# A hybrid attention layer on one core: the in-projection's dense keys normalized in one block, its finishing steps and sums dealt out anew

## The chip, the cores and the metric

The kernel runs on one core of one Trainium2 chip. The metric is device time in microseconds (us); the time before is the median of three runs. A core has TensorE (PE in the profile; its weight loads are PEld), VectorE (DVE), ScalarE (ACT), GpSimd (POOL) and SyncE (SP), which here issues nearly all DMAs. Each engine works through its own queue in order, and the queues meet at semaphores. PE writes its sums to PSUM, eight banks of 512 float32 for each of 128 partitions; what DVE, ACT and DMAs share otherwise is SBUF.

## The reference

One encoder layer on 1024 positions of width 1024. Cut to the part at hand:

```
proj = rms_norm(x, norm1_g) @ w_in            # (1024, 2304) -> qA 512 | kA 128 | vA 128 | qB 512 | kB 512 | vB 512
qa = apply_axial_rope(rms_norm(qa, qa_norm_g))   # 8 heads of 64
ka = apply_axial_rope(rms_norm(ka, ka_norm_g))   # 2 heads, used by 4 query heads each
out_a = softmax(qa @ ka.T / 8) @ va
out_b = dilated_mixture_attention(rms_norm(qb, qb_norm_g), rms_norm(kb, kb_norm_g), vb)
x = x + concat(rms_norm(out_a), rms_norm(out_b)) @ w_out
x = x + conv_ffn(rms_norm(x, norm2_g), w_up, conv_w, conv_b, w_down)
```

The keys and values of mixer A (kA, vA, 256 columns) are called dense here, those of mixer B dilated. qb_norm_g and kb_norm_g each multiply one side of the same inner product over the 64 elements of a head.

## The kernel before

All is in one function, `tile_encoder_layer`, which unrolls everything; its parts are small nested functions. Three arenas hold all data: `bigf` (float32), `bigr` (a float32 form for PE) and `ps` (PSUM); places are offsets such as `F_TMP` or `qab(t)`, and several stages use one place in turn. For the order of the work the kernel leaves it to a planner: from a planned time of each instruction and from what each reads and writes, it lays out the queue of each engine when the program is built. The text gives priorities, not the order: of the instructions that the planner takes to be ready, the one that comes first in the text goes first. At run time each queue is in order, whatever is late.

Products are made exact by splitting: an operand becomes a high part (ACT copy into `bigr`) and the rest (DVE subtraction), and three matmuls are added (L393 to L395: high x high, high x rest, rest x high).

The in-projection runs in these steps.

*Dense keys and values.* For each of eight tiles of 128 positions (`kv_proj`, L278 to L280) 24 matmuls give 256 columns in a PSUM bank (`kv_bank`: banks 0 to 3, then 2 and 3 in turn). `kv_stage1` squares the 128 key columns on ACT, sums them on DVE and takes the root on ACT (L291 to L294). `kv_stage2` finishes the reciprocal root (`newton`, L190 to L193, DVE), multiplies the keys (L302), builds a table of rope and gain (L304, POOL), multiplies by the cosines (L305), turns the halves (`rot`, L284, POOL), adds (L308), copies the values out of PSUM (L309, ACT) and writes the tile to DRAM (`kvscr`, L310). `x_prep` and `x_rest` between them transpose x (L179) and split it (L227, L228) and make the differences of halves (L249 to L253) that the products below need; `s_split` splits these.

*Four chunks of 512 columns*, in the order kB, vB, qA, qB (chunk 0 to 3). Each chunk is a 2 x 2 block product done with seven block products instead of eight, so there are 28 products (`prods`, numbered by `m`; the list at `prods` gives which of the seven, n, each one is). A product is 48 matmuls of 256 columns over four tiles, into one of three groups of two PSUM banks (`in_group`). Product n = 2 adds onto the group of n = 1, after ACT has copied that out (L408). `in_out(m)` takes a product out of PSUM and adds it to the block's outputs at `c_at`; at n = 6 four sums follow, two on DVE and two on POOL (L405 is the line of all sums). `w_prep(m + 2)` prepares the weights two products ahead: a difference of weight blocks (L366 DVE, L368, L370, L372 POOL), the high part (L376, ACT) and the rest (L377, DVE). `w_load` and `w_scale` (L353) bring the next chunk's weights; the places for the first half are used by every second chunk (`F_WA`).

*Finishing steps.* When a quarter of a chunk is complete, `done` returns its steps as a list: square (L463 to L465), root (L470 and `newton`), norm (L474), and then for kB the gain (L490, POOL) and the DMAs out (L494), for qA a table (L477, POOL), four turns (L284), cosine (L484) and add (L487); for vB a scaling on ACT (L444) and DMAs (L445). The main loop runs the whole list of a quarter after the product that follows its completion; of two quarters of qA three steps only, and all of qB's, are left for the attention that follows.

*Dense keys for attention.* In chunk 3 the tiles come back from DRAM two at a time (`kv_fetch`, L313), are split (`k_ready`: L319, L320), transposed by PE (L176) and copied (L326, L327); `v_ready` (L333) scales the values, `fill_k` (L337) fills constants. `a_prep(0)` prepares the first queries: its steps are `first`, four maxima `mx` (L582, L583) and `last`. Attention A then runs 16 groups (`a_main`), each of which takes the steps of the next group's `a_prep` by a plan, one number for each of its eight key tiles.

Names for the prediction's steps: `F_TMP` holds 1024 columns of scratch, `F_WA[1]` the first half of the weights of chunks 1 and 3 (and, before chunk 1, the places `F_KVT` and `F_CST`), `SM_R1` the positions' own norm factors for the values.

Of the kernel before, what the change touches and what calls it, by code (L numbers as in the profile page):

```python
# [20 lines left out]
HD = 64  # L21
# [37 lines left out]
R_KNA = 3072  # L59
# [6 lines left out]
F_KVT = O_F + 5120  # L66
F_ROPE = O_F + 8192
# [55 lines left out]
def tile_encoder_layer(ctx, tc, x, w_in, gains, outg, norm1_g, norm2_g, w_out, w_up, conv_w, conv_b,  # L123
# [164 lines left out]
    def kv_stage1(i):  # L288
        b = kv_bank(i)
        sq, t = F_TMP + 512 * (i % 2), SM_T + 48 * (i % 2)  # L290
        act(f(sq, 128), bank(b, 128), AF.Square)  # L291
        vec.tensor_reduce(f(t, 2), heads(f(sq, 128), 2), axis=AX.X, op=OP.add)
        vec.tensor_scalar(f(t + 8, 2), f(t, 2), 1.0 / HD, f(SM_E1 + i, 1), op0=OP.mult, op1=OP.add)
        act(f(t + 16, 2), f(t + 8, 2), AF.Sqrt)  # L294

    def kv_stage2(i):
        b = kv_bank(i)
        t = SM_T + 48 * (i % 2)
        qn, t1, t2 = [F_TMP + 512 * (i % 2) + 128 * u for u in (1, 2, 3)]
        tab, stg = F_KVT + 128 * (i % 2), F_KVT + 256 + 256 * (i % 2)  # L300
        newton(f(t, 2), f(t + 8, 2), f(t + 16, 2), f(t, 2))
        vec.tensor_tensor(heads(f(qn, 128), 2), heads(bank(b, 128), 2),  # L302
                          f(t, 2)[:, :, None].to_broadcast([128, 2, 64]), op=OP.mult)
        gp.tensor_tensor(f(tab, 128), f(F_ROPE + 128 * i, 128), f(O_GA + 128, 128), op=OP.mult)  # L304
        vec.tensor_tensor(heads(f(t1, 128), 2), heads(f(qn, 128), 2),  # L305
                          f(tab, 64)[:, None, :].to_broadcast([128, 2, 64]), op=OP.mult)
        rot(t2, qn, 2, tab)
        vec.tensor_tensor(f(stg, 128), f(t1, 128), f(t2, 128), op=OP.add)  # L308
        act(f(stg + 128, 128), bank(b, 128, 128), AF.Copy)  # L309
        dma(kvscr[i], f(stg, 256))  # L310

    def kv_fetch(u):
        dma(heads(f(F_TMP + 512 * (u % 2), 512), 2), kvscr[2 * u:2 * u + 2].rearrange("t p c -> p t c"))  # L313

    def k_ready(u):

        src = fp(F_TMP + 512 * (u % 2), [256, 2], [64, 2], [1, 64])
        kna = R_KNA + 512 * (u % 2)
        act(rp(kna, [256, 2], [128, 2], [1, 64]), src, AF.Copy)  # L319
        vec.tensor_tensor(rp(kna + 64, [256, 2], [128, 2], [1, 64]), src, rfp(kna, [256, 2], [128, 2], [1, 64]),  # L320
                          op=OP.subtract)
        b = next_tr()
        for i in range(4):
            tr_r(b, i, r(kna + 128 * i, 128))
# [4 lines left out]
    def v_ready(u):  # L329
        for i in range(2):  # L330
            tt = 2 * u + i
            v = fp(F_TMP + 512 * (u % 2) + 256 * i + 128, [64, 2], [1, 64])
            act(fp(F_VA + 132 * tt, [66, 2], [1, 64]), v, AF.Copy, scale=f(SM_R1 + tt, 1))  # L333
# [26 lines left out]
    def w_prep(m):  # L360
        if m >= len(prods):
            return
        c, n = prods[m]
        b11, b12, b21, b22 = [fp(w_buf(c, half) + 256 * u, [512, 4], [1, 256]) for half in range(2) for u in range(2)]
        if n == 5:
            vec.tensor_tensor(b11, b12, b11, op=OP.subtract)  # L366
        elif n == 7:
            gp.tensor_tensor(b12, b22, b12, op=OP.subtract)  # L368
        elif n == 6:
            gp.tensor_tensor(b11, b22, b11, op=OP.subtract)  # L370
        elif n == 4:
            gp.tensor_tensor(b11, b21, b11, op=OP.subtract)  # L372
        src = {2: b21, 3: b22, 7: b12}.get(n, b11)
        o = w_op(m)
        h = rp(o, [256, 4], [1, 256])
        act(h, src, AF.Copy)  # L376
        vec.tensor_tensor(rp(o + 1024, [256, 4], [1, 256]), src, rfp(o, [256, 4], [1, 256]), op=OP.subtract)  # L377
# [55 lines left out]
    later, deferred, n_done = [], [], [0]  # L433

    def done(c, t0, u, late=None):
# [5 lines left out]
        def v_out():  # L441
            for t in range(t0, t0 + 4):
                v = f(qab(t) + 256 * u, 256)
# [11 lines left out]
        sq = fp(so, [ss, 4], [64, 4], [1, 64])  # L455
        t, m = SM_T + 48 * (n_done[0] % 2), 1
# [5 lines left out]
        def square():  # L462
            act(sq, q3, AF.Square)  # L463
            vec.tensor_reduce(fp(t, [4, 4], [1, 4]), sq, axis=AX.X, op=OP.add)
# [24 lines left out]
        def gain():  # L489
            gp.tensor_tensor(q3, q3, fp(O_GB if kind == "qb" else O_GB + 64, [0, 4], [0, 4], [1, 64]), op=OP.mult)  # L490
# [7 lines left out]
        if kind == "kb":  # L498
            return [square, root, norm, gain, k_out]
# [30 lines left out]
    def late_consts():  # L530
        for g in (O_GA, O_GB):
# [35 lines left out]
    def a_prep(g):  # L567
# [3 lines left out]

        def first():
            q_nat(qab(b) + 256 * kv, 64, vec, 4, 512 * kv)
# [18 lines left out]
        return [first] + [lambda i=i: mx(i) for i in range(4)] + [last]  # L592
# [323 lines left out]
    for i in range(4):  # L916
# [5 lines left out]
        if i:  # L922
            kv_stage2(i - 1)
        kv_stage1(i)
# [7 lines left out]
    for m in range(len(prods)):  # L932
# [3 lines left out]
        if m < 2:  # L936
            for i in (4 + 2 * m, 5 + 2 * m):
# [5 lines left out]
                kv_stage2(i - 1)  # L943
                kv_stage1(i)
        if m == 1:
            kv_stage2(7)
            conv_consts()
            vec.tensor_scalar(v, f(SM_SS1, 8), 1.0 / D, EPS, op0=OP.mult, op1=OP.add)
            act(rt, v, AF.Sqrt)
            newton(f(SM_R1, 8), v, rt, f(SM_SS1, 8))  # L950
            w_load(1, 0)
# [8 lines left out]
        if m % 7 == 0 and 0 < c < 3:  # L960
# [4 lines left out]
        for d in ready:  # L965
            defer = d[0] == 3 or d[:2] == (2, 4)
            if d[0] < 3:
                take(done(*d), 3 if defer else 99)
            if defer:
                deferred.append(d)  # L970
        if last and n == 1:
            kv_fetch(0)
            kv_fetch(1)
        if last and n == 5:
            take(prep, 1)
        if last and n == 2:
            fill_k()
            for u in range(2):
                k_ready(u)
        if last and n == 7:  # L980
            gp.memset(fp(F_VA + 64, [66, 16]), 1.0)
            for u in range(2):
                v_ready(u)
                kv_fetch(u + 2)
        if last and n == 6:
            take(prep, 1)
            for u in range(2, 4):
                k_ready(u)
                v_ready(u)
        if last and n == 3:  # L990
            take(prep, 4)
    take(prep, 99)
    deferred += later
# [418 lines left out]
```

## Time and profile before

| | us |
|---|---|
| median of 3 runs | 1379.73 (1378.29 to 1380.36) |
| profiled execution, its own time | 1379.28 |
| span of the profiled execution | 1377.5 |
| mean granted TensorE clock | 0.988 |

The page counts busy time of each engine over the span, PE 1319.2 us of it. How to read the rows that follow in this document: a row of waits gives the engine and line that waited, what released it, the us in total, the times and the longest; a row of windows gives a stretch, its length, busy us of PE, PEld, DVE, ACT and POOL with the number of instructions, the granted clock (1.00 is full), the DMA engines' busy share and GB/s; a row of groups gives line, engine, operation, out<-in with shapes, the count, busy us, mean ns of one, and idle time of the engine ahead of them with its releasers; a row of the timeline gives start, duration, engine, line, operation, and in brackets the idle time before it. A line can be that of a helper, so L191 or L405 stands for many places.

The slices of the page show PE's clock and DMA load over the span; the in-projection is in the first seven of the forty:

```profile
PE   7898989999999999999998999999999999999998
PEld 6798989989999887887886788888888888888887
DVE  5986586774445677688558888778777888586664
```

### The profile page before, as it was taken

The numbers are of one execution on the slowest core, as the hardware profiler recorded it, in microseconds if no ns is written. First come the engines' busy times: TensorE is split into PE (matmuls) and PEld (weight loads), VectorE is DVE, ScalarE is ACT, GpSimd is POOL, SyncE is SP. The second block draws the span as 40 slices with busy tenths as digits, with TensorE's granted clock in tenths as the row PEclk, the third lists the DMA queues.
The fourth block names the chain that finished last, engine by engine and source line by source line (L and its number), as shares of the span: only waits on it lengthen the run. The fifth ranks groups of instructions, "written<-read, shape, count | busy, mean of one in ns | idle before, by whom it ended". The sixth has DMA issues, their size and how long they took to land.

```text
span 1377.5 us, 20282 instructions
## 1 busy us (share of the span) xinstructions
PE 1319.2 (96%) x7559; PEld 1141.6 (83%) x7559; DVE 988.2 (72%) x1634; ACT 671.5 (49%) x1066; POOL 515.3 (37%) x388
## 2 busy tenths in 40 slices
PE   7898989999999999999998999999999999999998
PEld 6798989989999887887886788888888888888887
DVE  5986586774445677688558888778777888586664
ACT  7744634554445656666344444444444445244331
POOL 2754354130001566651036455665565552200000
PEclk9999999999999999989999999999999999999999
DMA  7035303100000223234322222333223225797973
GB/s 245 16 116 138 78 9 87 30 9 1 1 1 9 83 71 102 82 109 137 107 70 84 91 94 92 102 112 112 103 100 115 85 100 176 280 293 239 295 232 112
DMA packets 117956, 148.61 MB, mean 108 GB/s; under 512 B 48809, under 2 KB 74849, under 8 KB 117857
## 3 DMA queue, kind: packets, MB, share of 16 engines
q1 hardware_dynamic: 116705, 144.17, 32.2%
q0 software_dynamic: 1152, 3.15, 0.9%
q8 instruction: 59, 0.97, 0.3%
q14 instruction: 40, 0.33, 0.1%
HBM read 113.47 MB, written 33.82 MB: 107 GB/s over the span
## 4 chain that ended last, share of the span: by engine, by line
PE 75%; DVE 12%; issue 3%; ACT 2%; POOL 1%; DMA 1%; DVEq 0%; ACTq 0%; SPq 0%; POOLq 0%
PE ps L1123 10%; PE ps L1124 9%; PE ps L1125 9%; PE ps L604 7%; PE ps L1239 5%; PE ps L1237 5%; PE ps L1238 5%; PE ps L609 2%; PE ps L582 2%; PE ps L847 2%; DVE bigf L707 2%; PE ps L610 2%; PE ps L849 2%; PE ps L848 2%; PE ps L393 2%
## 5 line engine op out<-in xcount | busy, mean ns | idle before, releaser
L1123 PE MATMUL ps<-bigr 128*128 128x512 f32 x616 | 241.7, 392 | 6.1 <-DVE bigf L1127 5.8
L1125 PE MATMUL ps<-bigr 128*128 128x512 f32 x616 | 240.5, 390 | 0.0
L1124 PE MATMUL ps<-bigr 128*128 128x512 f32 x616 | 240.2, 390 | 0.0
L1106 ACT ACTIVATE bigr<-bigf 128x512 fp32r<-128x512 f32 x154 | 93.0, 625 | 157.3 <-POOL bigf L1098 97.5
L1155 DVE SCALAR_TENSOR_TENSOR bigf<-bigf 128x768 f32<-128x768 f32 (+1 forms) x176 | 145.5, 885 | 27.0 <-ACT bigf L1153 27.0
L604 PEld LDWEIGHTS ps<-bigf 128*128 128x128 f32 x1024 | 138.7, 191 | 10.1
L1123 PEld LDWEIGHTS ps<-bigr 128*128 128x128 f32 x616 | 115.9, 188 | 34.5 <-DVE bigf L1127 10.0
L1217 ACT ACTIVATE bigr<-bigf 128x1024 fp32r<-128x1024 f32 x77 | 80.7, 1060 | 119.4 <-PE ps L1239 65.6
L393 PE MATMUL ps<-bigr 128*128 128x256 f32 x448 | 128.9, 288 | 7.8 <-ACT bigf L408 5.2
L1125 PEld LDWEIGHTS ps<-bigr 128*128 128x128 f32 x616 | 116.1, 188 | 24.3
L1107 DVE TENSOR_TENSOR bigr<-bigf,bigr 128x512 fp32r<-128x512 f32 x110 | 113.1, 1043 | 31.3 <-ACT bigr L1106 31.2
L1124 PEld LDWEIGHTS ps<-bigr 128*128 128x128 f32 x616 | 116.0, 188 | 23.5
L604 PE MATMUL ps<-bigf 128*128 128x65 f32 x1024 | 135.3, 267 | 0.0
L583 DVE TENSOR_REDUCE bigf<-ps 128x1 f32<-128x512 f32 x128 | 85.8, 689 | 64.7 <-PE ps L582 63.1
L394 PE MATMUL ps<-bigr 128*128 128x256 f32 x448 | 128.3, 287 | 0.0
L395 PE MATMUL ps<-bigr 128*128 128x256 f32 x448 | 128.1, 286 | 0.0
L612 ACT ACTIVATE bigf<-ps 128x512 f32<-128x512 f32 x128 | 76.0, 597 | 101.3 <-PE ps L610 99.7
L1238 PE MATMUL ps<-bigr 128*128 128x512 f32 x308 | 119.9, 389 | 0.0
L1237 PE MATMUL ps<-bigr 128*128 128x512 f32 x308 | 119.8, 389 | 0.0
L1239 PE MATMUL ps<-bigr 128*128 128x512 f32 x308 | 119.8, 389 | 0.0
L1218 DVE TENSOR_TENSOR bigr<-bigf,bigr 128x1024 fp32r<-128x1024 f32 x77 | 93.0, 1221 | 26.9 <-ACT bigr L1217 24.8
L1169 POOL TENSOR_TENSOR bigf<-bigf 128x512 f32<-128x512 f32 x44 | 69.1, 1591 | 90.3 <-DVE bigf L1160 66.0
(209 smaller groups left out, 3048.4 us busy)
## 6 DMA issues: line engine op xcount, KB each, us to landing
bigf<-w_down SPq DMA_DIRECT2D x99, 256.0 KB, 4.1
bigf<-w_up SPq DMA_DIRECT2D x44, 512.0 KB, 3.6
bigf<-gscr SPq DMA_DIRECT2D x77, 256.0 KB, 4.3
gscr<-bigf SPq DMA_DIRECT2D x33, 512.0 KB, 2.6
bigf<-w_in SPq DMA_DIRECT2D x8, 1024.0 KB, 6.7
bigf<-x SPq DMA_DIRECT2D x15, 512.0 KB, 8.0
bigf<-tmx SPq DMA_DIRECT2D x8, 672.0 KB, 5.0
bigf<-w_out SPq DMA_DIRECT2D x8, 512.0 KB, 3.6
```

The costliest lines, as they stand in the source:

```text
L393: mm(o, ah, wh, start=(k == 0 and t % 2 == 0 and n != 2), stop=False, skip_group_check=True)
L394: mm(o, ah, wl, start=False, stop=False, skip_group_check=True)
L395: mm(o, al, wh, start=False, stop=(k == 3), skip_group_check=True)
L604: mm(bank(ob, 65, 66 * i), f(slots[kt] + 128 * i, 128), f(F_VA + 132 * kt + 66 * kv, 65), start=(kt == 0 and i == 0), stop=(kt == 7), skip ...
L1107: (gp if n in (2, 4) else vec).tensor_tensor(rp(o + 512, [128, 4], [1, 128]), src, rfp(o, [128, 4], [1, 128]), op=OP.subtract)
L1123: mm(bank(b), wh, th, start=(k == 0 and n in (1, 5, 6, 7)), stop=False, skip_group_check=True)
L1124: mm(bank(b), wh, tl, start=False, stop=False, skip_group_check=True)
L1125: mm(bank(b), wl, th, start=False, stop=(k == 3), skip_group_check=True)
L1155: vec.scalar_tensor_tensor(f(a + o, n), f(i + d, n), w_, f(a + o, n), op0=OP.mult, op1=OP.add)
L1237: mm(o, ah, r(d, 512), start=(q == 0 and n in (1, 5, 2)), stop=False, skip_group_check=True)
L1238: mm(o, ah, r(d + 1024, 512), start=False, stop=False, skip_group_check=True)
L1239: mm(o, al, r(d, 512), start=False, stop=(q == NQ - 1), skip_group_check=True)
```

## The change

- **Dense keys.** `kv_stage1` and `kv_stage2` are gone. `kv_out(i)` copies all 256 columns of a tile out of PSUM with one ACT instruction and writes them to DRAM as they are. Later `k_fetch` reads all eight tiles' keys at once into `F_TMP` (at product 11), `k_norm` normalizes them and applies the gain (12), `k_turn` makes the turned part on POOL (13), `k_add` applies the cosines and adds (15). The scratch `F_KSQ` lies in `F_WA[1]`, so `w_load(3, 0)` moves from product 14 to product 16. `k_split` splits all keys at product 21; `k_ready(u)` only transposes and copies, for u = 0, 1 at product 23 and 2, 3 at 24. `R_KNA` moves to have room for all.
- **Dense values.** `v_fetch` reads them straight to their place with two DMAs of 64-element pieces at product 23, `v_scale` scales them with two DVE instructions at 24. `fill_k` moves from product 23 to 22. The values' norm factors `SM_R1` are computed at product 4 instead of 1.
- **Finishing steps dealt out.** A quarter's list is cut in pieces (square; root and norm; the next five; the rest), of which one runs per product (`going`). The squares of qA get a place of their own (`sq0`).
- **kB's gain** is no longer applied to the keys; `late_consts` multiplies it into qB's gain.
- **Second chunk's outputs** go to the upper half of `qab`, as those of chunk 3 do (`c_at`).
- **Sums on VectorE.** From chunk 1 on, the two sums at n = 6 and the weight differences for n = 7, 6 and 4 run on DVE instead of POOL.
- **a_prep** has its first step cut in two (`nat`, `first`), and the plan of `a_main` takes one more.

The diff, cut to its core:

```diff
-R_KNA = 3072
+R_KNA = 2048
+F_KSQ = O_F + 4096
...
+    def kv_out(i):
+        stg = F_KVT + 256 * (i % 3)
+        act(f(stg, 256), bank(kv_bank(i), 256), AF.Copy)
         dma(kvscr[i], f(stg, 256))
+    def k_fetch():
+        dma(heads(f(F_TMP, 1024), 8), kvscr[:, :, 0:128].rearrange("t p c -> p t c"))
+    def k_norm():
+        k3, t = heads(f(F_TMP, 1024), 16), F_KSQ + 1024
+        act(f(F_KSQ, 1024), f(F_TMP, 1024), AF.Square)
+        vec.tensor_reduce(f(t, 16), heads(f(F_KSQ, 1024), 16), axis=AX.X, op=OP.add)
+        vec.scalar_tensor_tensor(fp(t + 16, [2, 8], [1, 2]), fp(t, [2, 8], [1, 2]), 1.0 / HD,
+                                 fp(SM_E1, [1, 8], [0, 2]), op0=OP.mult, op1=OP.add)
+        act(f(t + 32, 16), f(t + 16, 16), AF.Sqrt)
+        newton(f(t, 16), f(t + 16, 16), f(t + 32, 16), f(t, 16))
+        vec.tensor_tensor(k3, k3, f(t, 16)[:, :, None].to_broadcast([128, 16, 64]), op=OP.mult)
+        vec.tensor_tensor(k3, k3, fp(O_GA + 128, [0, 16], [1, 64]), op=OP.mult)
+    def k_turn():
+        for ax in range(2):
+            for half in range(2):
+                gp.tensor_tensor(fp(F_KSQ + 32 * ax + 16 * half, [128, 8], [64, 2], [1, 16]),
+                                 fp(F_TMP + 32 * ax + 16 * (1 - half), [128, 8], [64, 2], [1, 16]),
+                                 fp(F_ROPE + 64 + 32 * ax + 16 * half, [128, 8], [0, 2], [1, 16]), op=OP.mult)
+    def k_add():
+        k4 = fp(F_TMP, [128, 8], [64, 2], [1, 64])
+        vec.tensor_tensor(k4, k4, fp(F_ROPE, [128, 8], [0, 2], [1, 64]), op=OP.mult)
+        vec.tensor_tensor(f(F_TMP, 1024), f(F_TMP, 1024), f(F_KSQ, 1024), op=OP.add)
+    def k_split():
+        src = fp(F_TMP, [64, 16], [1, 64])
+        act(rp(R_KNA, [128, 16], [1, 64]), src, AF.Copy)
+        vec.tensor_tensor(rp(R_KNA + 64, [128, 16], [1, 64]), src, rfp(R_KNA, [128, 16], [1, 64]), op=OP.subtract)
...
+    def v_fetch():
+        gp.memset(fp(F_VA + 64, [66, 16]), 1.0)
+        for kv in range(2):
+            dma(fp(F_VA + 66 * kv, [132, 8], [1, 64]),
+                kvscr[:, :, 128 + 64 * kv:192 + 64 * kv].rearrange("t p c -> p t c"))
+    def v_scale():
+        for kv in range(2):
+            v = fp(F_VA + 66 * kv, [132, 8], [1, 64])
+            vec.tensor_tensor(v, v, f(SM_R1, 8)[:, :, None].to_broadcast([128, 8, 64]), op=OP.mult)
...
+        eng = vec if c else gp
...
-            gp.tensor_tensor(b12, b22, b12, op=OP.subtract)
+            eng.tensor_tensor(b12, b22, b12, op=OP.subtract)
...
-        return qab(t0 if c else 4 - t0) + (512 if c == 3 else 0) + 256 * u
+        return qab(t0 if c else 4 - t0) + 512 * (c % 2) + 256 * u
...
-            add(gp, c12, c12, ua)
-            add(gp, c21, c21, ua)
+            add(vec if c else gp, c12, c12, ua)
+            add(vec if c else gp, c21, c21, ua)
...
+        sq0 = fp(qab(0) + 512, [1024, 4], [64, 4], [1, 64]) if kind == "qa" else sq
...
+        vec.tensor_tensor(f(O_GB, 64), f(O_GB, 64), f(O_GB + 64, 64), op=OP.mult)
...
-        if i:
-            kv_stage2(i - 1)
-        kv_stage1(i)
+        kv_out(i)
...
-        if m % 7 == 0 and 0 < c < 3:
+        if m in (7, 16):
             w_load(c + 1, 0)
...
-                take(done(*d), 3 if defer else 99)
+                ts = done(*d)
+                defer = d[:2] == (2, 4)
+                going.append([ts[:1], ts[1:3]] + [] if defer else [ts[:1], ts[1:3], ts[3:8], ts[8:]])
...
+        for g in list(going):
+            for t in g.pop(0):
+                t()
+            if not g:
+                going.remove(g)
+        if m == 11:
+            k_fetch()
+        if m == 12:
+            k_norm()
+        if m == 13:
+            k_turn()
+        if m == 15:
+            k_add()
         if last and n == 1:
-            kv_fetch(0)
-            kv_fetch(1)
+            k_split()
         if last and n == 5:
             take(prep, 1)
+            fill_k()
         if last and n == 2:
-            fill_k()
             for u in range(2):
                 k_ready(u)
+            v_fetch()
         if last and n == 7:
...
+            for u in range(2, 4):
+                k_ready(u)
+            v_scale()
+            take(prep, 1)
...
-        tail = a_main(g, prep, tail, late, (4, 4, 2, 2, 3, 2, 2, 2) if g == 15 else (1, 1, 1, 1, 1, 0, 1, 0),
+        tail = a_main(g, prep, tail, late, (4, 4, 2, 2, 3, 2, 2, 2) if g == 15 else (1, 1, 1, 1, 1, 1, 1, 0),
```

More of the change, by code (lines that the diff above doesn't have):

```diff
@@ L286, in rot @@
                              fp(tab + 64 + 16 * half, [0, nh], [32, 2], [1, 16]), op=OP.mult)
[L288 to L309, printed above, removed]
-        dma(kvscr[i], f(stg, 256))
@@ L327, in k_ready @@
         act(rp(R_KHA + 256 * u, [128, 2], [1024, 2], [1, 128])[0:64], pb[0:64], AF.Copy)
[L329 to L333, printed above, removed]
+    def v_fetch():
[7 more added lines that the diff above has]
+            vec.tensor_tensor(v, v, f(SM_R1, 8)[:, :, None].to_broadcast([128, 8, 64]), op=OP.mult)
     def fill_k():
@@ L431, in in_out @@
             fin(4, 0)
-    later, deferred, n_done = [], [], [0]
+    later, deferred, going, n_done = [], [], [], [0]
     def done(c, t0, u, late=None):
@@ L442, in v_out @@
             for t in range(t0, t0 + 4):
-                v = f(qab(t) + 256 * u, 256)
+                v = f(o + 1024 * (t - t0), 256)
                 act(v, v, AF.Copy, scale=f(SM_R1 + t, 1))
@@ L462, in square @@
         def square():
-            act(sq, q3, AF.Square)
-            vec.tensor_reduce(fp(t, [4, 4], [1, 4]), sq, axis=AX.X, op=OP.add)
+            act(sq0, q3, AF.Square)
+            vec.tensor_reduce(fp(t, [4, 4], [1, 4]), sq0, axis=AX.X, op=OP.add)
             vec.scalar_tensor_tensor(fp(t + 16 * m, [4, 4], [1, 4]), fp(t, [4, 4], [1, 4]), 1.0 / HD,
@@ L498, in done @@
         if kind == "kb":
-            return [square, root, norm, gain, k_out]
+            return [square, root, norm, k_out]
         return [square] + [root] * (late == 3), [norm, gain]
@@ L570, in a_prep, with nat @@
         ql = R_QLA + 512 * (g % 2)
+        def nat():
+            q_nat(qab(b) + 256 * kv, 64, vec, 4, 512 * kv)
         def first():
-            q_nat(qab(b) + 256 * kv, 64, vec, 4, 512 * kv)
             t = next_tr()
@@ L590, in last @@
             act(r(ql, 512), bank(t), AF.Copy)
-        return [first] + [lambda i=i: mx(i) for i in range(4)] + [last]
+        return [nat, first] + [lambda i=i: mx(i) for i in range(4)] + [last]
     def a_main(g, prep, tail, late, plan, late_plan):
@@ L942, in tile_encoder_layer @@
                 s_split(5, i - 4)
-                kv_stage2(i - 1)
-                kv_stage1(i)
+                kv_out(i)
         if m == 1:
-            kv_stage2(7)
             conv_consts()
+        if m == 4:
             vec.tensor_scalar(v, f(SM_SS1, 8), 1.0 / D, EPS, op0=OP.mult, op1=OP.add)
@@ L950, in tile_encoder_layer @@
             newton(f(SM_R1, 8), v, rt, f(SM_SS1, 8))
+        if m == 1:
             w_load(1, 0)
@@ L965, in tile_encoder_layer @@
         for d in ready:
-            defer = d[0] == 3 or d[:2] == (2, 4)
             if d[0] < 3:
-                take(done(*d), 3 if defer else 99)
-            if defer:
+                ts = done(*d)
+                defer = d[:2] == (2, 4)
+                going.append([ts[:1], ts[1:3]] + [] if defer else [ts[:1], ts[1:3], ts[3:8], ts[8:]])
+            if d[0] == 3 or d[:2] == (2, 4):
                 deferred.append(d)
+        for g in list(going):
[11 more added lines that the diff above has]
+            k_add()
         if last and n == 1:
-            kv_fetch(0)
-            kv_fetch(1)
+            k_split()
         if last and n == 5:
             take(prep, 1)
+            fill_k()
         if last and n == 2:
-            fill_k()
             for u in range(2):
                 k_ready(u)
+            v_fetch()
         if last and n == 7:
[L981 to L984, printed above, removed]
+            for u in range(2, 4):
+                k_ready(u)
+            v_scale()
+            take(prep, 1)
         if last and n == 6:
             take(prep, 1)
-            for u in range(2, 4):
-                k_ready(u)
-                v_ready(u)
         if last and n == 3:
@@ L992, in tile_encoder_layer @@
     take(prep, 99)
+    assert not going
     deferred += later
```

15 lines of the change are left out of this document (4 added, 11 removed).

## The prediction, made before the change was run

> **What bounds the kernel now.** I read the page first, then TensorE's waits over the first 420 us, then the windows, and last the queues of the engines that ended the waits. Durations come from the profiled execution, 1379.28 us, of which the span is 1377.5 and 1.8 lies around it; the median of the three runs, 1379.73, is 0.45 above, which I leave aside.
>
> ```profile
> PE 1319.2 (96%) x7559; PEld 1141.6 (83%) x7559; DVE 988.2 (72%) x1634; ACT 671.5 (49%) x1066; POOL 515.3 (37%) x388
> L393 PE MATMUL ps<-bigr 128*128 128x256 f32 x448 | 128.9, 288 | 7.8 <-ACT bigf L408 5.2
> ```
> TensorE (PE) is busy 1319 of 1377 us; no matmul is removed, so only its idle time, and the time in which it runs slowly, can be won. L393 has 448 matmuls, 16 for each of the 28 products, so products can be counted off in the trace. I number them 0 to 27, seven to a chunk.
>
> ```profile
> core 0: us, PE busy (x) PEld busy (x) DVE busy (x) ACT busy (x) POOL busy (x), PEclk, DMA share, GB/s
> 30.00:74.00 44.00, 35.96 (x272) 34.64 (x273) 43.12 (x96) 30.05 (x64) 28.04 (x26) 0.92 0.05 17
> 74.00:114.00 40.00, 34.78 (x286) 34.38 (x286) 36.04 (x41) 20.30 (x29) 19.45 (x10) 0.99 0.39 122
> 114.00:201.00 87.00, 87.00 (x716) 87.00 (x716) 55.82 (x56) 41.64 (x63) 40.56 (x30) 0.98 0.28 74
> 201.00:240.00 39.00, 33.39 (x245) 31.32 (x244) 27.92 (x45) 18.21 (x32) 14.96 (x14) 0.91 0.29 83
> 240.00:1378.00 1138.00, 1107.88 (x5909) 935.39 (x5909) 809.73 (x1351) 539.71 (x837) 405.63 (x297) 0.99 0.34 110
> ```
> The in-projection is all ahead of about 237 us. From 30 to 114 VectorE (DVE) is busy 79 of 84 us and PE idles 13; from 114 to 201 PE never idles and DVE has 31 us to spare; from 201 to 240 PE idles 5.6. Nothing behind 240 is changed but where one piece of the query preparation is cut, so I let that stretch keep its length. The idle time by its releaser:
>
> ```profile
> PE ps L393 <- ACT bigf L408: 5.2, 1, 5.2
> PE ps L278 <- ACT bigf L309: 5.0, 2, 3.9
> PE ps L179 <- DMA bigf<-x: 4.4, 1, 4.4
> PE ps L176 <- DVE bigf L191: 3.6, 1, 3.6
> PE ps L278 <- ACT bigr L267: 2.9, 1, 2.9
> PE ps L176 <- DVE bigr L320: 1.7, 1, 1.7
> PE ps L179 <- DVE bigf L250: 1.7, 1, 1.7
> PE ps L393 <- ACT bigr L376: 1.4, 1, 1.4
> PE ps L179 <- ACT bigf L247: 1.2, 1, 1.2
> PE ps L393 <- ACT bigf L309: 1.2, 1, 1.2
> ```
> Without the two first loads (4.4 and 2.9, untouched) that is 21.0 us. Three of the stops cost more than themselves:
>
> ```profile
> 60.80:66.00 5.20, 5.17 (x25) 5.17 (x26) 5.20 (x14) 3.66 (x8) 2.33 (x4) 0.52 0.09 28
> 113.50:119.50 6.00, 5.92 (x37) 5.92 (x38) 5.90 (x6) 2.83 (x4) 4.21 (x2) 0.72 0.52 127
> 120.90:126.90 6.00, 6.00 (x52) 6.00 (x51) 1.19 (x2) 3.19 (x6) 2.40 (x1) 1.00 0.37 82
> 207.50:213.50 6.00, 5.95 (x33) 5.98 (x34) 3.81 (x7) 4.45 (x9) 1.94 (x1) 0.58 0.17 44
> ```
> The third row is the undisturbed rate: 52 matmuls in 6.00 us, 0.115 each, clock 1.00. Behind the 3.9 us stop 25 take 5.17 at clock 0.52 (2.3 lost), behind the 5.2 us stop 37 take 5.92 at 0.72 (1.7 lost), behind the 1.7 and 3.6 us stops 33 take 5.95 at 0.58 (2.2 lost; I take 2.0, since some of them are short transposes). So 21.0 + 6.0 = 27 us is all that this change can win.
>
> **The change, part by part.** *Start, up to product 0.* kv_stage1's root goes, and with it an ACT table load that stands ahead of L247:
>
> ```profile
> L294 ACT ACT_TABLE_LOAD x1 | 1.3, 1283 | 0.0
> L308 DVE TENSOR_TENSOR bigf<-bigf 128x128 f32<-128x128 f32 x8 | 4.7, 581 | 1.0 <-POOL bigf L284 1.0
> L190 DVE RECIPROCAL bigf<-bigf 128x2 f32<-128x2 f32 x8 | 1.3, 157 | 1.1 <-ACT bigf L294 1.1
> ```
> The load of 1.28 covers the whole 1.2 us stop at L247; it comes back at the first root of chunk 0's keys, where ACT has room (20.3 busy of 40). At product 0's stop (1.4, ACT's copy L376) ACT loses small squares and roots and gains a 256-wide copy for each tile, so I count 0.5 of it. Together **1.7**.
>
> *Dense key stage, 30 to 74.* Nine kinds of DVE instructions (first L308, last L190 of the rows between, 4.7 + 4.5 + 3.2 + 2.6 + 2.4 + 2.3 + 2.2 + 1.5 + 1.3 = 24.7 us, times of waiting for POOL included) go, and four small POOL ones per tile. What is left, kv_out, is one ACT copy and one DMA as soon as kv_proj ends. PSUM bank 2 or 3 is then free about 0.5 us behind its last matmul instead of behind the whole DVE and POOL chain. Hence the 5.0 (L309 ahead of kv_proj 6 and 7), the 1.2 (L309 ahead of product 3) and the 2.3 of slow clock go; the L250 stop (1.7) shrinks, because L250 stood behind a normalization step in DVE's queue: 1.4 of it. Sum **9.9**. Late next would be the halves' splits (s_split) for products 2 and 3; DVE, at 43 of 44 us now, would have some 28 of 36, so I keep 1.5 back for it. kv_out waits for kv_proj on ACT with w_prep's copies behind it; PE works on another product meanwhile.
>
> *Product 9.* It accumulates on product 7's sums and must wait for ACT's copy L408:
>
> ```profile
> 77.30 1.06 ACT L463 ACTIVATE bigf<-bigf 128x1024 f32<-128x1024 f32 x1 [3.58 <-DVE bigf L308]
> ...
> 108.81 1.06 ACT L463 ACTIVATE bigf<-bigf 128x1024 f32<-128x1024 f32 x1 [3.88 <-DVE bigf L192]
> 112.40 0.22 ACT L470 ACTIVATE bigf<-bigf 128x16 f32<-128x16 f32 x1 [2.53 <-DVE bigf L465]
> 112.52 1.01 ACT L408 ACTIVATE bigf<-ps 128x1024 f32<-128x1024 f32 x1
> ```
> and DVE's queue in the same time:
>
> ```profile
> 91.54 3.42 DVE L405 TENSOR_TENSOR bigf<-bigf 128x1024 f32<-128x1024 f32 x1
> 105.27 2.31 DVE L191 TENSOR_TENSOR bigf<-bigf 128x16 f32<-128x16 f32 x1
> 107.50 1.21 DVE L405 TENSOR_TENSOR bigf<-ps,bigf 128x1024 f32<-128x1024 f32 x1
> ```
> L408 ended at 113.5 and PE had waited 5.2, so product 8 ended at 108.3; at 48 x 0.12 = 5.8 a product, product 7 ended near 102.5 and product 6 near 96.7. L408 stands behind the last key block's square and root, and those behind DVE: the sum at 107.50 could have run when product 6 ended. DVE was 10.8 us behind, much of it waiting: a 16-element multiplication takes 2.31 us and a sum 3.42 while POOL works.
>
> ```profile
> L405 POOL TENSOR_TENSOR bigf<-bigf 128x1024 f32<-128x1024 f32 x8 | 23.1, 2916 | 16.3 <-DMA bigf<-w_in 10.6 <-DVE bigf L405 5.7
> L490 POOL TENSOR_TENSOR bigf<-bigf 128x1024 f32<-128x1024 f32 x4 | 10.5, 2620 | 18.7 <-DVE bigf L474 13.9 <-DVE bigf L465 4.8
> L372 POOL TENSOR_TENSOR bigf<-bigf 128x1024 f32<-128x1024 f32 x4 | 10.0, 2505 | 24.2 <-DVE bigr L377 23.0 <-DVE bigf L193 1.2
> L474 DVE TENSOR_TENSOR bigf<-bigf 128x1024 f32<-128x1024 f32 x8 | 9.8, 1221 | 0.3 <-DVE bigf L193 0.2
> L191 DVE TENSOR_TENSOR bigf<-bigf 128x16 f32<-128x16 f32 x8 | 7.3, 918 | 0.2
> ```
> Gone: four gains (L490, 2.6 each on POOL), and from chunk 1 on the POOL differences of w_prep, which already run here for products 10 and 11. Moved: a full-width operation is 1.22 on DVE against 2.5 to 2.9 on POOL. Laying out DVE's work from the end of product 4 (0) by these rows, with chunk 0's two POOL sums still in its way: the sums, three key blocks and the splits for products 7 to 9 bring the last block's root to about 19 and L408 to 20, product 9 may start at 23. So the 5.2 and the 1.7 go, **6.9**, with 3 us in hand; I keep 1.0 back. Chunk 1's outputs in the upper half also no longer wait for the keys' DMAs.
>
> The Trainium skill, in Perfetto Trace Analysis, section Optimizing Scalar/DVE Operations, notes that GPSIMD and VectorE share an SBUF read port, so that moving work between those two might not help. By that rule the moved sums bring nothing and the 6.9 stays lost, which is rival (a). The trace agrees that the two block each other (2.31 us for 16 elements), but has the moved operation at less than half its POOL time.
>
> *Chunks 1 to 3.* DVE gains two sums and three differences per chunk, 15 x 1.22 = 18.3, and the key block: reduction, root's steps (0.9 and less each), two products, two in k_add, the split, some 9; it loses waits (L191 is 0.92 on average and 2.31 beside POOL). On 56 busy of 87 that makes at most 83, and PSUM groups are reused two products (11.7 us) later, so a backlog of some 6 to 8 us around products 18 to 21 stays covered; I keep 1.0 back. k_turn and the two fetches are not in the trace:
>
> ```profile
> L284 POOL TENSOR_TENSOR bigf<-bigf 128x128 f32<-128x128 f32 x23 | 11.2, 519 | 15.4 <-DVE bigf L474 13.0 <-DVE bigf L405 2.3
> bigf<-kvscr SPq DMA_DIRECT2D x4, 256.0 KB, 2.8
> bigf<-w_in SPq DMA_DIRECT2D x8, 1024.0 KB, 6.7
> ```
> One of k_turn's four handles 256 elements: between 0.5 (L284, 128) and 2.5 (L372, 1024); I take 0.9, nearer L284. k_fetch moves twice the 256 KB of a row of 2.8, so 2.8 to 5.6, with product 11's stage to itself; ACT's square waits for it and the copies out of PSUM stand behind, with two products of slack. Both end on DVE or POOL, so the cost on the path is 0, and at worst 5.6 less 11.7 of cover, still 0. A gain from them is excluded, nothing on PE waits for this work today before product 23. w_load(3, 0) moves on SP's queue from product 14 to 16, behind k_add: 6.7 to landing, then scaling, against product 21 five products (29 us) later.
>
> *End of the in-projection.* k_ready's transposes waited for L320 and, behind DVE's L191, for its second half. The split now stands at product 21, two products ahead of the transposes, with no v copies beside it. 1.7 + 3.6 + 2.0 = **7.3**; I keep 1.0 back for DVE's backlog. The v fetches (64-element pieces) have the time to the first weighted sum, over 20 us.
>
> Sum: 1.7 + 9.9 + 6.9 + 7.3 = 25.8, less 1.5 + 1.0 + 1.0 + 1.0 = 4.5 kept back: 21.3. 1379.3 - 21.3 = **1358.0 us**.
>
> **The rivals.** (a) *Product 9's stop stays.* ACT's queue is laid out at build time by planned readiness, not by the text: the row at 77.30 is the first key block's square, which the text puts behind product 4, and product 4 was yet to start. So handing out the pieces over products may leave the square and root ahead of L408, and only DVE's lighter load would help; and that doesn't come if the moved sums and POOL's remaining ones block each other as before. 6.9 stays: 1379.3 - (21.3 - 5.9) = 1363.9. Chance 0.14.
>
> (b) *The key split comes late.* If DVE's queue at product 21 holds a cosine step that waits for POOL's eight turns (8 x 0.52 = 4.2), the 7.3 stay: 1379.3 - (21.3 - 6.3) = 1364.3. Chance 0.08.
>
> (c) *ACT holds the dense stage.* If ACT's splits, not DVE, set products 1 to 3, half of 9.9 stays: 1379.3 - (21.3 - 5.0) = 1363.0; with (a) or (b) 1369. Against it: ACT is busy 30 of 44. Chance 0.08.
>
> (d) *Slower: VectorE becomes the bound of chunks 1 to 3.* If its backlog exceeds the two products that a PSUM group is held, every moved operation lands on PE's path: 18.3 + 9 = 27.3, and 1358.0 + 27.3 = 1385. It decides from a backlog of 11.7 us, against the 10.8 seen now with POOL in the way. For it: DVE queues are in order. Against: 31 us spare in 114 to 201. Chance 0.06.
>
> **How the numbers follow.** Forecast 0.64, (a) 0.14, (b) 0.08, (c) 0.08, (d) 0.06. The likeliest case alone spans 1353 (all 25.8 won) to 1363. The range goes to 1369 for (a) to (c) and their pairs, and a little below 1353 for idle time that I counted as kept: 1352 to 1369. A difference under 0.2%, 2.8 us, could hardly be told from none by this measurement; that needs (a), (b) and (c) together and more: 0.03. Slower 0.06, faster 0.91.
>
> **What would show it.** Right: the waits on L309, L408, L320 and L191 are gone from PE's list; the clock stays near 1.00 from 30 to 230; product 3 starts some 11 us earlier, product 27 ends near 215; DVE is under 80% from 30 to 74. Wrong: a long PE wait on ACT's copy ahead of product 9 (a); transposes waiting for the key split (b); PE waits on ACT splits before 70 us (c); waits of L393 on DVE in chunks 1 to 3 (d).

## The result and the profile after

The changed kernel takes 1359.14 us (median of 4 runs, 1358.56 to 1359.84), the kernel before 1380.05 beside it: a ratio of 0.9849 (95% interval 0.9836 to 0.9862), 20.9 us less. The profiled span went from 1377.5 to 1356.5 us. The page's first line, and TensorE's waits over the first 420 us (engine and line that waited, releaser, us in total, times, longest):

```profile
PE 1310.1 (97%) x7559; PEld 1134.7 (84%) x7559; DVE 978.7 (72%) x1587; ACT 668.9 (49%) x1041; POOL 461.2 (34%) x349
```

```profile
PE ps L180 <- DMA bigf<-x: 4.5, 1, 4.5
PE ps L279 <- ACT bigr L268: 2.9, 1, 2.9
PE ps L177 <- ACT bigr L333: 2.2, 2, 1.8
PE ps L599 <- DVE bigf L600: 1.7, 2, 0.9
PE ps L405 <- ACT bigf L291: 1.2, 2, 0.6
PE ps L626 <- ACT bigf L629: 1.1, 1, 1.1
```

Line numbers have moved by some: L405 to L407 are the products (L393 to L395 before), L420 the copy that product 9 waits for (L408), L417 the sums (L405), L177 the transposes (L176). The two first loads stay; of the other eight waits, 21.0 us, none is left under its old name. Three small ones are new: the key transposes wait for the copy of the set before them (2.2), product 2 waits twice for kv_out (1.2), the first scores of attention for the exponential (1.1). The maxima's wait for the last ones' reduction has grown to 1.7 from the 0.8 that it was before:

```profile
PE ps L582 <- DVE bigf L583: 0.8, 2, 0.5
```

The windows, by the same five stages:

```profile
30.00:63.00 33.00, 31.82 (x266) 31.45 (x265) 30.87 (x40) 29.73 (x52) 21.52 (x11) 1.00 0.14 44
63.00:98.00 35.00, 35.00 (x294) 35.00 (x294) 30.58 (x49) 21.08 (x29) 4.75 (x2) 1.00 0.39 109
98.00:182.00 84.00, 84.00 (x705) 84.00 (x703) 63.85 (x78) 42.52 (x61) 13.35 (x18) 1.00 0.32 85
182.00:215.00 33.00, 30.16 (x228) 28.76 (x226) 29.34 (x38) 12.80 (x20) 10.04 (x15) 0.95 0.28 82
215.00:1357.00 1142.00, 1106.51 (x5916) 933.98 (x5916) 810.61 (x1353) 540.51 (x838) 408.17 (x299) 1.00 0.33 109
```

The columns are as before: length, busy us of PE, PEld, DVE, ACT, POOL, then PE's clock. PE never idles from 63 to 182 us, and the clock is 1.00 from 30 to 182. (The slice rows shown with the profile before are busy shares of PE, PEld and DVE; the clock is read from the windows.) The stage that took 44 us (30 to 74) takes 33. VectorE is busy 30.9 of 33 us there, so it is nearly as full as before (94% against 98%), only for a shorter time.

Where the 21.0 us came from can be counted off. The time from the end of one product to the end of the next, from the records of the three product lines, 48 to a product (an undisturbed one takes 5.76):

```
                 end of 3    9     16     22     23     24     25    27   end of 27   from there on
before              79.3  12.71   5.76   5.76   5.76  14.30   5.76  7.81    236.6       1140.9
after               66.5   5.76   5.76   5.76   5.76   6.46  10.64  7.75    212.6       1143.9
undo_deal           65.6   5.76   5.76   5.76   5.76  11.91   6.45  7.75    213.0       1145.3
undo_sums           65.3   6.50  13.64   5.76  12.32   6.46   9.44  7.83    225.5       1145.9
diffs_back          66.9   6.51   5.76  11.11   6.88   6.46  10.09  7.76    219.7       1144.4
undo_places         66.2   5.76   5.76   5.76   5.76   6.46   8.24  7.85    210.1       1143.7
undo_gain           65.7   5.76   5.76   8.42   6.14   6.46  11.74  7.75    216.0       1143.8
dense_alone         65.5  13.68  13.39   5.76   7.05  10.48   6.46  7.82    228.4       1144.0
rest_alone2         77.5   6.39   5.76   5.76   5.76  13.00   5.76  7.75    227.1       1142.7
gain_alone          79.3   7.92   5.76   5.76   5.76  13.42   5.76  7.82    230.9       1142.9
fill_later          66.2   5.76   5.76   5.76   5.76   6.47   6.49 12.41    212.9       1142.7
exp_early           66.2   5.76   5.76   5.76   5.76   6.46  10.81  7.76    212.6       1143.3
tail_mix            66.3   5.76   5.76   5.76   5.76   6.47   6.49 12.10    212.7       1143.5
```

The first two rows: 12.9 us were won up to product 3, 6.95 at product 9, 3.0 around products 24 and 25, the rest in small pieces; 24.0 at the end of the in-projection. Behind it 3.0 were given back. The other rows are the experiments.

### The profile page after: what moved, and what is told of

It reads as the page before. It is cut to its first block, busy times and chain, and to the rows that moved or that the text cites. A ratio compares the mean times of both kernels' runs of the same rounds, so it can differ in the third digit from the quotient of the medians.

```text
span 1356.5 us, 20119 instructions
## 1 busy us (share of the span) xinstructions
PE 1310.1 (97%) x7559; PEld 1134.7 (84%) x7559; DVE 978.7 (72%) x1587; ACT 668.9 (49%) x1041; POOL 461.2 (34%) x349
## 4 chain that ended last, share of the span: by engine, by line
PE 72%; DVE 15%; ACT 5%; issue 3%; POOL 3%; DMA 2%; SPq 0%; ACTq 0%; DVEq 0%; POOLq 0%
PE ps L1150 8%; PE ps L621 8%; PE ps L1151 8%; PE ps L1152 8%; PE ps L1266 5%; PE ps L1265 5%; PE ps L1264 5%; PE ps L626 3%; PE ps L599 2%; DVE bigf L1182 2%; PE ps L627 2%; PE ps L864 2%; DVE bigf L724 2%; PE ps L866 2%; PE ps L865 2%
## 5 line engine op out<-in xcount | busy, mean ns | idle before, releaser
L621 PEld LDWEIGHTS ps<-bigf 128*128 128x128 f32 x1024 | 138.8, 191 | 10.3
L621 PE MATMUL ps<-bigf 128*128 128x65 f32 x1024 | 134.0, 267 | 0.0
L405 PE MATMUL ps<-bigr 128*128 128x256 f32 x448 | 127.9, 286 | 1.2 <-ACT bigf L291 1.2
L407 PE MATMUL ps<-bigr 128*128 128x256 f32 x448 | 127.3, 284 | 0.0
L629 ACT ACTIVATE bigf<-ps 128x512 f32<-128x512 f32 x128 | 75.9, 597 | 92.8 <-PE ps L627 91.0
L600 DVE TENSOR_REDUCE bigf<-ps 128x1 f32<-128x512 f32 x128 | 85.4, 689 | 24.2 <-PE ps L599 23.0
```

What stands on the lines that cost most here:

```text
L405: mm(o, ah, wh, start=(k == 0 and t % 2 == 0 and n != 2), stop=False, skip_group_check=True)
L407: mm(o, al, wh, start=False, stop=(k == 3), skip_group_check=True)
L621: mm(bank(ob, 65, 66 * i), f(slots[kt] + 128 * i, 128), f(F_VA + 132 * kt + 66 * kv, 65), start=(kt == 0 and i == 0), stop=(kt == 7), skip ...
```

## The experiments

Theory 1 is the prediction's: VectorE lagged behind because GpSimd's operations blocked it, and product 9 waited for that lag. Theory 2 is rival (a): the order of ScalarE's queue, with the finishing steps run whole, was the cause.

**Dealing out undone.**

```diff
-                ts = done(*d)
-                defer = d[:2] == (2, 4)
-                going.append([ts[:1], ts[1:3]] + [] if defer else [ts[:1], ts[1:3], ts[3:8], ts[8:]])
+                take(done(*d), 3 if d[:2] == (2, 4) else 99)
```

> The changed kernel with the finishing steps run whole again, not dealt out. Theory 1 (product 9 was late because VectorE lagged 10.8 us behind, blocked by GpSimd's key work, gains and sums): no stop ahead of product 9 comes back, 1358 to 1361 us. Theory 2 (the order of ScalarE's queue did it, and dealing out changed it): the stop of 5.2 and its slow clock come back, 1364 to 1367 us.

1360.04 us, as theory 1 said; product 9 doesn't stop. So handing out the steps isn't what freed it, and theory 2 falls in that form. Whether the order of ScalarE's queue matters is not decided by this run: here too the last block's root stands behind the copy, at 93.46 us against 90.39. The copy's place in the changed kernel, in the timeline of ScalarE (start, us, then the instruction, and in brackets what it waited for):

```profile
90.17 1.06 ACT L476 ACTIVATE bigf<-bigf 128x1024 f32<-128x1024 f32 x1 [1.16 <-DVE bigf L192]
91.14 1.01 ACT L420 ACTIVATE bigf<-ps 128x1024 f32<-128x1024 f32 x1
92.04 1.05 ACT L388 ACTIVATE bigr<-bigf 128x1024 fp32r<-128x1024 f32 x1
94.45 0.22 ACT L483 ACTIVATE bigf<-bigf 128x16 f32<-128x16 f32 x1 [1.36 <-DVE bigf L478]
```

The last block's square (L476) still stands ahead of the copy L420, its root (L483) is now behind. The copy ends at 92.2; product 8 ended at 95.25. That leaves 3.1 us in hand.

**Sums and weight differences of chunks 1 to 3 back on GpSimd**, and then the differences alone.

```diff
-        eng = vec if c else gp
+        eng = gp
...
-            add(vec if c else gp, c12, c12, ua)
-            add(vec if c else gp, c21, c21, ua)
+            add(gp, c12, c12, ua)
+            add(gp, c21, c21, ua)
```

> The changed kernel with the sums and weight differences of chunks 1 to 3 on GpSimd again. Theory 1: VectorE is blocked some more, two differences in the time ahead of product 9 cost it at most 2.4 us of the 3.1 us of margin there, so product 9 doesn't stop; 1358 to 1362 us. Rival (the moved sums carry the gain of 6.9 us): product 9 stops again, 1365 to 1368 us. At the key transposes (1.8 us wait now, released by ScalarE, which waited 7.9 us for a difference on VectorE): if that difference's place on VectorE is the cause, this wait shrinks and 2 to 3 us come back, and the run could be as fast as the changed kernel or faster.

1373.55 us, 14.4 more than the changed kernel. Both expectations are wrong. Product 9 loses only 0.7 us, although square, root and copy stand in the order of the kernel before (root at 93.40, copy at 93.51 us): with less of GpSimd in its way VectorE comes in time in that order as well. But products 16 and 23 lose 7.9 and 6.6, and neither had a stop before the change. The waits of this run have

```profile
PE ps L405 <- ACT bigf L420: 9.7, 3, 5.6
```

in three places. The one at product 16, in the timelines of POOL, DVE, ACT and PE in this run:

```profile
127.58 3.69 POOL L312 TENSOR_TENSOR bigf<-bigf 128x256 f32<-128x256 f32 x4 [3.69 <-issue]
131.24 1.29 POOL L490 TENSOR_TENSOR bigf<-bigf 128x512 f32<-128x512 f32 x1
132.49 3.36 POOL L382 TENSOR_TENSOR bigf<-bigf 128x1024 f32<-128x1024 f32 x1
```

```profile
131.31 2.31 DVE L318 TENSOR_TENSOR bigf<-bigf 128x1024 f32<-128x1024 f32 x1 [2.72 <-POOL bigf L312]
133.65 3.29 DVE L319 TENSOR_TENSOR bigf<-bigf 128x1024 f32<-128x1024 f32 x1
136.86 1.21 DVE L417 TENSOR_TENSOR bigf<-ps,bigf 128x1024 f32<-128x1024 f32 x1
```

```profile
138.10 1.71 ACT L456 ACTIVATE bigf<-bigf 128x256 f32<-128x256 f32 x4 [9.09 <-DVE bigf L417]
139.72 1.00 ACT L420 ACTIVATE bigf<-ps 128x1024 f32<-128x1024 f32 x1
```

```profile
140.77 0.58 PE L405 MATMUL ps<-bigr 128*128 128x256 f32 x1 [5.61 <-ACT bigf L420]
```

This is the key block's own chain. L318 and L319 are the two steps of k_add. The first waits in VectorE's queue for k_turn (L312), and both then stretch from 1.2 to 2.3 and 3.3 us beside GpSimd's table and weight difference. Behind them stands the sum of product 13 (L417, ready at 123.6, run at 136.9), behind that ScalarE's scaling of the values (L456), and behind that the copy L420. That is more than the two products for which a PSUM group may be held.

The stop at product 23 has another chain. There a cosine step of qA (L497) waits 2.46 us for GpSimd's turns (L285) at 176.60 and then takes 3.40 us beside the weight difference L382. Behind it stand the sum of product 20 (L417, ready at 171.8, run at 183.5), a square, a root, and at 185.87 the copy L420.

The Trainium skill, in SBUF — State Buffer, section Who interferes with whom, says that VectorE and GpSimd share one port pair under an exclusive lock. The trace agrees: L382 takes 3.36 us on GpSimd here against 2.4 to 2.5 for such a difference in the kernel before, and L319 3.29 us on VectorE against 1.2. By the rows above L382 ends 2.2 us after L318, and L319 1.1 us after L382: each takes about its own length once the other is done.

> The changed kernel with the weight differences of chunks 1 to 3 on GpSimd again, the two sums of each chunk still on VectorE. undo_sums (both back) stops products 16 and 23 for 7.9 and 6.5 us. If the differences carry it (one stands between the two steps of k_add there, and holds VectorE 3.3 us): both stops remain, 1370 to 1374. If the sums carry it: both are gone, 1358 to 1362.

1366.18 us, 7.0 more than the changed kernel and 7.4 less than with the sums back as well, between the two expectations. Products 16 and 23 don't stop as they did, but product 22 now loses 5.4 us:

```profile
PE ps L406 <- DVE bigr L389: 3.6, 1, 3.6
```

It waits for its own weights' rest (L389), which is made from a difference and runs at 173.82, behind the same cosine step (2.45 us of waiting for the turns, then 3.37). So sums and differences are worth about the same, and they are worth it in chunks 2 and 3, not at product 9.

**Chunk 1's outputs in the lower half again.**

```diff
-        return qab(t0 if c else 4 - t0) + 512 * (c % 2) + 256 * u
+        return qab(t0 if c else 4 - t0) + (512 if c == 3 else 0) + 256 * u
```

> The changed kernel with chunk 1's outputs in the lower half again, where they wait for the keys' DMAs. Theory 1: ScalarE waits for these DMAs some us around products 8 to 10, but no group of PSUM is wanted back in that time; within 1 us of the changed kernel, 1358 to 1361. Rival (the places removed a wait that TensorE felt): 1362 or more, with a TensorE wait on ScalarE's copies between products 9 and 12.

1356.67 us, 2.5 less than the changed kernel and below both expectations; 2.4 of it is at product 25 (8.24 us against 10.64), and why isn't settled. In this run chunk 1's outputs go over keys whose write to DRAM now comes later in the text, so part of the dilated keys is changed; the work is the same. The free places win no time by themselves: dealing out the steps needs them for its data.

**The dilated keys' gain back on GpSimd**, and the folded gain alone on the kernel before.

```diff
-        vec.tensor_tensor(f(O_GB, 64), f(O_GB, 64), f(O_GB + 64, 64), op=OP.mult)
...
-            return [square, root, norm, k_out]
+            return [square, root, norm, gain, k_out]
```

> The changed kernel with the gain of the dilated keys as four operations of 2.4 to 2.6 us on GpSimd again. Theory 1: they block VectorE by up to 2 us each ahead of product 9, more than the margin of 3.1 us if two or more fall before the copy; a stop of 0 to 3 us, 1359 to 1363. Theory 2 (queue order alone): no change, 1358 to 1360.

1362.58 us, 3.4 more; within theory 1's range, but not where it expected. Product 9 doesn't stop; products 22 and 25 lose 2.7 and 1.1 more.

> The kernel before with one edit: the dilated keys' gain folded into the queries' gain, so four operations of 2.6 us leave GpSimd around products 5 to 9. Theory 1 (VectorE's lag behind GpSimd is what stops product 9; moved sums or the missing gain each suffice): the 5.2 us wait on ScalarE's copy falls under 1 us, 1372 to 1375. Rival (several parts are needed, or the queue order is it): the wait keeps 3 us or more, 1377 to 1380.

1375.60 us against 1379.48, ratio 0.9972 (0.9962 to 0.9982). Between the two expectations: product 9's wait falls from 5.2 to

```profile
PE ps L393 <- ACT bigf L408: 1.9, 1, 1.9
```

and the product from 12.71 to 7.92 us, so the four gains alone are 4.8 of the 6.95. Square, root and copy keep the order of the kernel before in this run (root at 109.1, copy at 109.2 us), so this part is not the queue's order. With undo_gain, where the moved weight differences do it without the gains, this bears out theory 1: less of GpSimd beside VectorE frees the copy, and it doesn't matter much which part goes.

**The two halves of the change alone.** dense_alone is the changed kernel with the four edits above undone together; rest_alone is the kernel before with those four made.

> Only the dense keys' part of the change (one copy a tile, keys normalized at once from DRAM, values scaled later, the root of the values' norm and the weight load moved); pieces not dealt out, sums on GpSimd, gain and chunk 1's places as before. Theory 1a (the dense part is worth 13 us up to product 3 and 4 at the key transposes, and product 9's 6.9 belong to the rest): 1363 to 1366, with a stop ahead of product 9. Theory 1b (VectorE's lag at product 9 was left over from the key work too, so the dense part alone removes most of the stop): 1357 to 1361.

1374.24 us, a ratio of 0.9963 (0.9950 to 0.9976): only 5.1 us under the kernel before, and above both expectations. The dense stage gives 13.8 us up to product 3 (1.3 of them by shorter waits for the first loads), but product 9 takes 13.68 us, 1.0 more than before, and products 16 and 23 stop anew (7.6 and 1.3):

```profile
PE ps L405 <- ACT bigf L420: 11.4, 3, 5.3
PE ps L177 <- DVE bigf L192: 2.0, 1, 2.0
```

So the lag at product 9 wasn't left over from the key work (1b falls).

> The kernel before with all of the change but the dense keys' part. Theory 1a: product 9's stop goes (6.9), the stops at the dense stage and at the key transposes stay: 1371 to 1375. Theory 1b: product 9's stop stays at least in part: 1375 to 1380.

rest_alone took 1373.06 us; it lacked the squares' own place, so it was run again with it:

> As rest_alone, with the place of its own for qA's squares, which that run lacked (there the square of a later quarter overwrote turned queries, so part of qA was changed). If this place only guards data: within 1 us of rest_alone's 1373.1, with no wait of more than 0.5 us ahead of product 9 and all of the dense stage's and key transposes' waits.

1371.55 us, a ratio of 0.9946 (0.9931 to 0.9961), 7.9 under the kernel before, and 1.5 under rest_alone where 1 was allowed. Product 9 loses 0.6 us; the waits of the dense stage stay but for the 1.2 on L309 ahead of product 3, and those of the transposes are 4.4 us in place of 5.3:

```profile
PE ps L278 <- ACT bigf L309: 5.0, 2, 3.9
PE ps L176 <- DVE bigr L320: 4.4, 1, 4.4
...
PE ps L393 <- ACT bigf L408: 0.4, 1, 0.4
```

Alone the halves win 5.1 and 7.9 us, together 20.9. The 8 us between are in the main the stops at products 16 and 23 (7.6 and 1.3), which only dense_alone has of the four (before, changed and the two halves); the other differences, up to 3 us each, nearly cancel. The one at product 16 has the key block's chain as in undo_sums: the sum of product 13 was ready at 131.0 and ran at 143.7. So the dense keys' block makes that stop, and the sums and differences on VectorE prevent it.

**The new wait at the key transposes.** In the changed kernel ScalarE's and VectorE's queues there are

```profile
178.09 1.03 ACT L422 ACTIVATE bigf<-ps 128x1024 f32<-128x1024 f32 x1
186.96 1.06 ACT L388 ACTIVATE bigr<-bigf 128x1024 fp32r<-128x1024 f32 x1 [7.85 <-DVE bigf L382]
187.93 1.00 ACT L424 ACTIVATE bigf<-ps 128x1024 f32<-128x1024 f32 x1
188.83 0.59 ACT L332 ACTIVATE bigr<-ps 128x512 fp32r<-128x512 f32 x1
189.31 0.58 ACT L333 ACTIVATE bigr<-ps 64x512 fp32r<-64x512 f32 x1
```

```profile
182.21 0.64 DVE L348 TENSOR_SCALAR bigr<-bigf 64x512 fp32r<-64x512 f32 x1
182.87 1.39 DVE L487 TENSOR_TENSOR bigf<-bigf 128x1024 f32<-128x1024 f32 x1
184.27 1.20 DVE L348 TENSOR_SCALAR bigr<-bigf 64x512 fp32r<-64x512 f32 x2
185.48 1.39 DVE L382 TENSOR_TENSOR bigf<-bigf 128x1024 f32<-128x1024 f32 x1
```

The copies out of the transposes (L332, L333) stand behind L388, which waits 7.85 us for the weight difference L382, now on VectorE and behind the constant fill (L348).

```diff
         if last and n == 5:
             take(prep, 1)
-            fill_k()
         if last and n == 2:
+            fill_k()
```

> The changed kernel with the constant fill of the keys (four VectorE instructions) emitted at product 23 again, behind the weight difference for product 25. If this fill and what stands around it make that difference late, which holds ScalarE for 7.9 us and the key transposes for 1.8 + 0.4 us: the waits on ScalarE's copies there shrink to under 0.5 and 2 to 3.5 us are won up to product 25, 1355.5 to 1357. If VectorE is simply behind by then: within 1 us of the changed kernel.

1358.25 us, the same as the changed kernel by its interval (0.9834 to 0.9864). The cause is shown: the transposes' wait is gone and product 25 takes 6.49 us instead of 10.64. But product 27 takes 12.41 instead of 7.75, because the maxima of the first queries now come early enough to wait for VectorE:

```profile
PE ps L599 <- DVE bigf L417: 3.2, 1, 3.2
```

The 4.2 us only moved two products on: the wait of the first expectation, the time of the second.

**The exponential's table load.** In the changed kernel a load of 1.28 us stands ahead of the first exponential (L629). This run issues one exponential earlier.

> The changed kernel with one exponential of one column (times zero, result unused) on ScalarE during product 27, so that the table load stands ahead of the first attention group. If the load of 1.28 us is what the first score matmul waits for (1.1 us): that wait goes, 1357.5 to 1358.5. If VectorE's maxima follow at once: within 0.5 us of the changed kernel.

```diff
+            act(f(SM_T + 103, 1), f(SM_MC, 1), AF.Exp, scale=0.0)
```

1357.08 us, ratio 0.9836 (0.9820 to 0.9853). The first scores' wait falls from 1.1 to

```profile
PE ps L626 <- ACT bigf L629: 0.4, 1, 0.4
```

and the maxima's wait (L599 on L600) falls from 1.7 to 0.3. From the end of product 27 to the end of the first 256 of attention A's 1024 weighted sums (L621) it takes 57.5 us instead of 59.1, and 57.6 in tail_mix, which has the same exponential. So 1.5 us are won there. The median is 2.1 us under the changed kernel's, but the intervals of the two ratios overlap, so for the whole run a gain isn't shown.

**All three at once.** The constant fill later, the early exponential, and chunk 3's two sums back on GpSimd.

> The changed kernel with the constant fill at product 23, the early exponential, and chunk 3's two sums on GpSimd again, where nothing is left for GpSimd to do. If VectorE's four sums in a row hold the maxima for 3.2 us in fill_later: that wait goes, the key transposes' wait stays away, the table load is covered; 2 to 5 us under the changed kernel, 1354.5 to 1357. Rival (GpSimd's sums block VectorE as much as they relieve it): 1357 to 1359.

1358.01 us, 0.9846 (0.9831 to 0.9862): the rival's value. The wait ahead of product 27 stays:

```profile
PE ps L599 <- DVE bigf L417: 2.7, 1, 2.7
```

There the sum that the maxima wait for needs one of the two that went to GpSimd, where it took 3.34 us. No version that computes the same and beats the changed kernel clearly over the whole run was found. That one more order of these sums (the one that the maxima need first, the other two on GpSimd) would win the 4 us wasn't tried.

## Why the prediction came out right

1358.0 us were predicted, 1359.14 measured. Step by step, from the product ends above:

- **Start and dense stage: 1.7 + 9.9 = 11.6, with 1.5 kept back.** Measured 12.9: 2.3 by the end of product 0, whose stop went whole and not by 0.5, and 10.5 from there on. The mechanism was right: the waits on L309, L247 and L250 are gone, the clock is 1.00. The 1.2 on L309 was counted as won and came back as product 2's two waits of 0.6 on kv_out; by `kv_bank` and `in_group` product 2 is the one that writes to the banks of the last two tiles. The slow clock was worth more than the 2.3 that were counted: 0.92 over 44 us is some 3.5 us (an estimate). VectorE was to be under 80% busy from 30 to 74 and is busy 40.4 of 44 us; that sign failed, without a wait of TensorE that shows it. dense_alone shows the part by itself (13.8, with the 1.3 of the first loads).
- **Product 9: 6.9, with 3 us in hand.** Measured 6.95, with 3.1 in hand. GpSimd in VectorE's way was the cause; the prediction put gains and moved operations together, and gain_alone puts 4.8 on the gains. The layout was not right in its order: the root was put at about 19 us behind the end of product 4, ahead of the copy, and ran at 22, behind it. So it is luck that the copy still had 3 us in hand, but little hangs on the order: undo_sums has the old one and loses 0.7. The forms of rival (a) fall: undo_deal has no stop, though the square does stand ahead of the copy, as that rival said.
- **The rule of the Trainium skill that moving work between the two engines might not help** (Perfetto Trace Analysis, section Optimizing Scalar/DVE Operations), which the prediction ties to rival (a), isn't borne out here: with the dense keys' block in place the moved operations are worth 14.4 us (undo_sums).
- **Chunks 1 to 3: no cost, "still 0" at worst, 1.0 kept back.** The result was 0, but the reason was incomplete. It set the key block against VectorE's spare time and not against the chain from k_turn through k_add, a sum and the scaled values to a copy. With the sums and differences on GpSimd that chain costs 7.9 us at product 16 (undo_sums). The 6.6 us at product 23 are a second chain that the prediction had only in rival (b), and there for the key split: qA's cosine step behind GpSimd's turns. The prediction credited the moved operations to product 9, where having them back costs 0.7; what they do is to make room for the key block and for qA's finishing steps.
- **Key transposes: 7.3, with 1.0 kept back.** Mis-sized: 3.0 at products 24 and 25. The old waits on L320 and L191 went as said, but the copies out of the transposes became late, behind the weight difference that had been moved to VectorE. Rival (b) named this place with another cause (a cosine step); its price was 6.3.
- **Behind the in-projection: no change.** It lost 3.0 us. Of these 1.9 are in the first quarter of attention A (59.1 us against 57.2), where the waits came to 2.8 against 0.8 before: 1.1 at the exponential, whose table load was covered before, and 1.7 at the maxima. exp_early puts 1.5 of it on the load. In the second half of attention A 0.5 more are lost, which wasn't settled, nor was why the load is no longer covered. The rest is no more than the spread: from the end of attention A to the feed-forward network the traces of the changed kernel and of fill_later and undo_sums, which have the same text there, take 270.8, 269.6 and 271.6 us.
- **Rival (d), slower,** didn't occur: VectorE is busy 64 of 84 us from 98 to 182. Its condition, a backlog of more than 11.7 us, does occur in undo_sums, where the operations are not moved: the sum that was ready at 123.6 ran at 136.9.

From the 25.8 us counted gross: 1.3 more up to product 3, 4.3 less at the transposes, 3.0 given back, 1.2 more in small pieces between, which makes the 21.0 of the spans. The 4.5 us kept back had the right size, but most of it went at places or by causes that the prediction had not named. So the mechanisms of the first two parts carried the forecast, and that the sum came within 1.2 us is in part luck.

## What to carry to other kernels

Parts of a change need not add: here 5.1 and 7.9 us alone are 20.9 together, because one part's new work would have made the stops that the other part's moves prevent. In a kernel with in-order queues, ask of a moved block what it waits for in the middle, and follow the queue behind that wait until it reaches a buffer that the bounding engine wants back. A late stop that is cured may come back a few steps later, if the engine that caused it is still behind.

## What the runs showed of the hardware

A stop need not be long to cost clock. In the changed kernel the transposes wait 1.8 and 0.4 us, with little between, and the window around them has

```profile
188.00:194.50 6.50, 4.25 (x24) 4.00 (x24) 6.50 (x10) 6.50 (x12) 0.33 (x1) 0.75 0.01 3
195.00:201.00 6.00, 6.00 (x54) 6.00 (x53) 5.01 (x9) 2.74 (x5) 0.78 (x2) 1.00 0.59 183
```

a granted clock of 0.75, and 1.00 just behind. Product 25 took 10.64 us there for 2.2 us of waiting, 6.49 with the wait gone (fill_later), so the stop cost nearly twice its length.
